# Expert input rows on ScalarE's DMA queue, and three placements around a mixture of experts

## The chip, the cores and the metric

The kernel runs on one core of one Trainium2 chip. The metric is the device time of one execution in microseconds (us), as the median of several runs. PE is TensorE, DVE VectorE, ACT ScalarE, POOL GpSimd and SP SyncE. Each of them has an instruction stream of its own, which it works through in order; SP does nothing here but issue DMAs, and ACT and POOL issue DMAs among their other instructions.

## The reference, cut to what matters

Two layers run over 256 latent and 256 context tokens of width 1024. Each layer has attention, an output projection, a layer norm, and then a mixture of 16 experts, two of which work on each token:

```
x   = layer_norm(ALPHA * x + (1 + gate1) * o, ln1_g, ln1_b)       # o: output projection
u   = x * (1 + scale2) + shift2                                   # input rows of the experts
affinity = sigmoid(u @ w_router);  best group, then its top 2 experts;  gate = affinity / their sum
f   = sum over the two experts of  gate * ((silu(u @ w1[e]) * (u @ w3[e])) @ w2[e])
x   = layer_norm(ALPHA * x + (1 + gate2) * f, ln2_g, ln2_b)
```

In layer 0 both streams go through the experts (512 tokens). In layer 1 only the latent tokens do (256), and only they are returned.

## The kernel before, in words

**Tokens and experts.** A layer's tokens stand in tiles of 128 rows: `n_out` is 4 in layer 0 and 2 in layer 1. An expert works on a block of at most `CAP` tokens, 96 in layer 0 and 64 in layer 1, whose rows it fetches from DRAM by their numbers; an expert with more tokens than that would be worked off inside an `If` (L1354), which is not entered with these inputs. The weights of the experts, 6 MB each, stream through SP's queue from beginning to end (L1302, pieces of 1 MB; L1293, two halves of one).

**End of the output projection.** For each tile of tokens `residual` (L915 to L917) makes the sum `z` out of the projection `oacc` and the stream `xs`. `post_norm` then takes the statistics (`BN_STATS`, L245, and on ACT the root of the variance, `sd<-mv`, L251, called `keep["root"]` in the code), forms the experts' input rows `u2` on DVE (L924, L943; the profile calls this tile `u`), writes them to the DRAM tensor `u2d` by a DMA (L944), and forms the normalised row `xs` on ACT (L942). Two DVE operations (L946, L949) turn that row into the residual that the experts' results are to be added to, and a DMA on ACT's queue (L950) writes it to the DRAM tensor `ysum`. `router` transposes `z` on PE, copies the transposes out of PSUM on ACT (`zt<-ztp`, L961) and multiplies them with the router's weights into `lgt`; L971 to L973 on DVE make the affinities' arguments `aff` of it. For the last tile a dummy sigmoid (L940) loads ACT's function table beforehand. The sigmoid of all affinities is one instruction (L1007), and it waits for the last tile's `aff`.

**Routing and the first gather.** DVE works out who goes where (up to `posm`, the place of each token at each expert). For expert 0 the one-hot matrix `oh` (L1125) is multiplied with token numbers on PE (`ix`, L1132 and L1134), DVE makes indices of it (`ii`, L1148, `keep["found"]`), POOL zeroes `xg` (L1150) and gathers the rows of `u2d` (L1151). The gather must wait for all writes to `u2d`. Behind it on POOL stand the gate parts (L1087 and its neighbours, which fill `auxg`), and behind them PE's `ix` sums of the gates (L1134). DVE's residual operations that are listed as `late` stand behind `ii`. Some weight loads wait for a mark that POOL sets behind a gather.

**The stages of a mixture.** For each expert: up-projection (`ha` for the first 64 slots, L1178, and in layer 0 `hb` for the other 32, L1184), gating on ACT (SiLU, L1205 and L1209) and DVE (L1206 and L1210), transposes of the gated rows on PE (`tp`, L1163) that ACT copies out (`gT`, L1166), down-projection (`ya`, `yb`), gate and addition to `ysum` by a scattering DMA (L1247).

**Its tail.** Behind the last expert's up-projection the rows of `ysum` are read back (`yu`, L1454). ACT casts each tile's row to a head (`parts`, L1456), and DVE (tile 0) or POOL (the others, in layer 0) subtracts the head from the row (L1457), so that head and rest can be summed exactly on PE together with the last expert's result (`racc`, L1488 and L1498). Dummy products (`warm`, L202, into `spare`) stand on PE ahead of the transposes of the last gated rows.

**What sets the order.** Each engine's instructions stand in the order in which a scheduler places them at build time; `order(a, b, ...)` puts a behind b, and `tc.high_priority()` takes a stretch ahead. In addition each DMA issued by SP or ACT takes one of eight completion semaphores in turn, and waits until the last DMA on the same semaphore has landed (the `DMAHW` waits in the listings below). A DMA issue that waits holds up all that stands behind it on its engine.

Of the kernel before, what the change touches and what calls it, by code (L numbers as in the profile page):

```python
# [17 lines left out]
F32 = mybir.dt.float32  # L18
# [4 lines left out]
AF = mybir.ActivationFunctionType  # L23
ALU = mybir.AluOpType
# [85 lines left out]
def layers(ctx: ExitStack, tc: tile.TileContext, x_in, x_ctx, c_in, w_in, w_out, w_ada, rows_in, lnv, sink, gains, rpbp,  # L110
# [344 lines left out]
    def pre_moe(l, sb, sr):  # L455
# [5 lines left out]
        with ExitStack() as st, ExitStack() as su:  # L461
# [458 lines left out]
            def post_norm(t, z):  # L920

                _, gg, bb = mods[t // 2]
                mean, rstd = stats([z[:, h] for h in half])
                u2 = tmp.tile([P, D], F32, tag="u2", name="u2")  # L924
                V.scalar_tensor_tensor(out=u2[:, half[0]], in0=z[:, half[0]], scalar=mean, in1=gg[:, half[0]],
                                       op0=ALU.subtract, op1=ALU.mult)
                if t < n_out - 1:
                    y, nmr = rstd()
                    for n in range(2):
                        if n:  # L930
                            V.scalar_tensor_tensor(out=u2[:, half[n]], in0=z[:, half[n]], scalar=mean, in1=gg[:, half[n]],
                                                   op0=ALU.subtract, op1=ALU.mult)
                        V.scalar_tensor_tensor(out=u2[:, half[n]], in0=u2[:, half[n]], scalar=y, in1=bb[:, half[n]],
                                               op0=ALU.mult, op1=ALU.add)
                    S.activation(out=xs[:, t], in_=z, func=AF.Identity, scale=y, bias=nmr)
                else:
                    V.scalar_tensor_tensor(out=u2[:, half[1]], in0=z[:, half[1]], scalar=mean, in1=gg[:, half[1]],
                                           op0=ALU.subtract, op1=ALU.mult)
                    y, nmr = rstd()
                    order(S.activation(out=sm.tile([P, 1], F32, tag="sd", name="sigmoid"), in_=epsc, func=AF.Sigmoid),  # L940
                          keep["root"], mybir.DependencyClass.NoSync)
                    S.activation(out=xs[:, t], in_=z, func=AF.Identity, scale=y, bias=nmr)  # L942
                    V.scalar_tensor_tensor(out=u2, in0=u2, scalar=y, in1=bb, op0=ALU.mult, op1=ALU.add)  # L943
                keep["u2 written"] = nc.sync.dma_start(u2d[t * P:(t + 1) * P], u2)  # L944

                d = V.scalar_tensor_tensor(out=xs[:, t], in0=xs[:, t], scalar=ALPHA, in1=lg, op0=ALU.mult, op1=ALU.mult)  # L946
                if t in (2, n_out - 1):
                    keep.setdefault("late", []).append(d)
                V.scalar_tensor_tensor(out=xs[:, t], in0=lb, scalar=ALPHA, in1=xs[:, t], op0=ALU.mult, op1=ALU.add)  # L949
                S.dma_start(ysum[l][t * P:(t + 1) * P], xs[:, t])  # L950
                return z, mean, y

            def router(t, z, mean, y):
                r = t // 2
                for hf in range(2):
                    tp = ps.tile([P, 512], F32, tag="s", name="ztp")
                    for k in range(4):
                        kt = hf * 4 + k
                        T.transpose(tp[:, k * P:(k + 1) * P], z[:, kt * P:(kt + 1) * P], ident)
                    zt = tmp.tile([P, 512], F32, tag="zt", name="zt")  # L960
                    d = S.copy(zt, tp)  # L961
                    if hf and t == n_out - 1:
                        order(d, keep["root"], mybir.DependencyClass.NoSync)
                    for k in range(4):
                        kt = hf * 4 + k
                        keep["logits"] = T.matmul(lgt[:, t * NE:(t + 1) * NE], zt[:, k * P:(k + 1) * P], wsc[:, r, kt],
                                                  start=(kt == 0), stop=(kt == 7))

                lo = aff[:, t]
                ms = sm.tile([P, NE], F32, tag="ms", name="ms", bufs=2)  # L970
                V.tensor_scalar(out=ms, in0=wsum[:, 0, r], scalar1=mean, scalar2=None, op0=ALU.mult)  # L971
                V.tensor_tensor(out=lo, in0=lgt[:, t * NE:(t + 1) * NE], in1=ms, op=ALU.subtract)
                V.scalar_tensor_tensor(out=lo, in0=lo, scalar=y, in1=wsum[:, 1, r], op0=ALU.mult, op1=ALU.add)  # L973
# [128 lines left out]
    class Experts:  # L1102
# [53 lines left out]
        def transposed(self, src, n, tag, after=None):  # L1156

            kk, cap, pool = n // P, self.cap, self.m1 if tag == "x" else self.m2
            out_ = pool.tile([P, kk, cap], F32, tag=tag + "T", name=tag + "T")
            for a in range(0, kk, 4):  # L1160
                tp = self.ps2.tile([P, 512], F32, tag="tp", name="tp")
                for k in range(4):
                    d = T.transpose(tp[:, k * P:k * P + cap], src[:cap, (a + k) * P:(a + k + 1) * P], ident[:cap, :cap])  # L1163
                    if after is not None:
                        order(d, after, mybir.DependencyClass.NoSync)
                (V.tensor_copy if a else S.copy)(out_[:, a:a + 4], tp.rearrange("p (k c) -> p k c", k=4)[:, :, :cap])  # L1166
            return out_

        def side_by_side(self, acc, x, kts, w, n):
# [30 lines left out]
        def gated(self, acc):  # L1200
# [2 lines left out]
            n = min(self.cap, 64)  # L1203
            hs = self.m2.tile([P, DE], F32, tag="hs", name="hs")
            S.activation(out=hs[:n], in_=a[:n], func=AF.Silu)  # L1205
            V.tensor_tensor(out=hs[:n], in0=hs[:n], in1=a[64:64 + n], op=ALU.mult)  # L1206
            for hf in range(2) if b is not None else ():
                o, c, k = hs[64:self.cap, hf * 256:hf * 256 + 256], 64 * hf, self.cap - 64
                S.activation(out=o, in_=b[c:c + k, 0:256], func=AF.Silu)  # L1209
                V.tensor_tensor(out=o, in0=o, in1=b[c + 32:c + 32 + k, 0:256], op=ALU.mult)  # L1210
            return hs

        def result(self, ht, pieces):
# [36 lines left out]
    def moe(l, ringb, gen, rt, u2d, aff, nt, sb, ahead):  # L1250
        cap = CAP[l]
        with ExitStack() as st:
# [197 lines left out]
                     for pool, tag in ((ringu, "wu"), (ringu, "wu"), (ringb[0], "wb"), (ringu, "wu"))[:nt]]  # L1450
            parts = [u[:, i * D:i * D + D] for u in parts for i in range(2)]
            g = ex.gates(toks[-1][1])
            heads, rests = [], []
            for t in range(nt):  # L1454
                keep["sums"] = nc.sync.dma_start(ys[t], ysum[l][t * P:(t + 1) * P])
                heads.append(S.copy(parts[2 * t], ys[t]))  # L1456
                rests.append((G if t in REST_G[l] else V).tensor_tensor(out=parts[2 * t + 1], in0=ys[t],  # L1457
                                                                     in1=parts[2 * t].bitcast(F32),
                                                                     op=ALU.subtract))
            spare = ps1.tile([P, 512], F32, tag="hb", name="spare")  # L1460
            warm(WARM[4], spare, keep["product"])
            acc = ex.result(ex.transposed(hs, DE, "g", after=keep["warm"]), piece)
            last_product = keep["product"]
            ahead(order)
            yl = ringb[1].tile([P, 2048], F32, tag="wb", name="yl")
# [160 lines left out]
```

## Time and profile before

| | us |
|---|---|
| three runs | 1144.89, 1145.07, 1151.78 |
| median | 1145.07 |
| profiled execution | 1139.29 |
| its span in the trace | 1137.5 |
| PE busy | 1017.5 (89%) |
| layer 0: end of the output projection and routing | 313 to 343 |
| layer 0: experts | 343 to 615 |
| layer 0: tail | 615 to 640 |
| layer 1: end of the output projection and routing | 850 to 882 |
| layer 1: experts | 882 to 1102 |

The profiled execution is 5.78 us shorter than the median of the runs, and 1.8 us longer than its own span. A row of the timeline gives start and duration in us, engine, line, operation and tiles (out<-in), and in brackets how long the engine stood idle ahead of it and what ended that. A row of the windows gives the busy time of each engine in a stretch, then the granted TensorE clock (1.00 is full speed), the busy share of the DMA engines (which can come out a little above 1) and GB/s. Layer 1's experts run at the pace of the weight loads, layer 0's at the pace of PE.

### The profile page before, as it was taken

To read this page: it belongs to the slowest core of one execution; us is meant where nothing else is said; L and a number is where in the kernel's file an instruction comes from. 1 tells how busy PE (TensorE), PEld (TensorE's weight loads), DVE (VectorE), ACT (ScalarE), POOL (GpSimd) and SP (SyncE) were. 2 spreads that over 40 slices of the span, in tenths; PEclk is the share of its full clock that TensorE was granted. 3 is DMA by queue.
4 is the path that set the end of the run, shared out by engine and by line. 5 is a ranking of instruction groups with operands and counts; after the bars stand their busy time and mean duration, and the time that the engine had idled before them with its cause. 6 is when DMAs were issued, how large, how long until landed. Compare 5 with 4: busy or idle time off the path is not lost. (4 is left out here: it accounts for less than half of the span.)

```text
span 1137.5 us, 21098 instructions
## 1 busy us (share of the span) xinstructions
PE 1017.5 (89%) x8683; PEld 597.6 (53%) x8684; DVE 522.4 (46%) x1221; ACT 332.6 (29%) x688; POOL 257.0 (23%) x238
## 2 busy tenths in 40 slices
PE   6998999999959999999996799989985999778775
PEld 4676767677844444444442577667773334222222
DVE  2424756665962344444434634566875222111115
ACT  1324568465221011011111533456631101000002
POOL 3000000100013433433324200001002455434142
PEclk9998999999968999999999899999996999989987
DMA  9845353866798999999995326674398999999992
GB/s 315 319 154 172 135 150 107 310 223 249 279 395 281 374 376 363 368 369 338 353 379 203 115 94 212 212 239 149 139 402 301 367 391 398 398 390 389 407 388 82
DMA packets 65617, 320.93 MB, mean 282 GB/s; under 512 B 14702, under 2 KB 18894, under 8 KB 35048
## 3 DMA queue, kind: packets, MB, share of 16 engines
q1 hardware_dynamic: 48576, 289.21, 66.9%
q0 software_dynamic: 11136, 23.30, 7.8%
q10 hardware_dynamic: 5800, 6.97, 1.8%
q8 instruction: 71, 1.16, 0.4%
q14 instruction: 34, 0.28, 0.1%
HBM read 310.40 MB, written 18.15 MB: 289 GB/s over the span
## 5 line engine op out<-in xcount | busy, mean ns | idle before, releaser
L1178 PE MATMUL ha<-w,xT 128*32 128x512 f32 (+1 forms) x1512 | 252.5, 613 | 17.7 <-DMA w<-in_w_dram 17.2
L1178 PEld LDWEIGHTS ha<-w,xT 128*32 128x32 f32 (+1 forms) x1512 | 74.8, 123 | 161.9 <-issue 122.4
L1205 ACT ACTIVATE hs<-ha 64x512 f32<-64x512 f32 x32 | 18.9, 590 | 403.6 <-PE ha L1178 403.6
L1178 PE MATMUL ya<-w,gT 128*32 128x512 f32 (+1 forms) x768 | 124.8, 597 | 3.2 <-DVE y L1225 1.6
L222 PE MATMUL pj<-wl,u 128*128 128x512 f32 (+2 forms) x256 | 97.8, 383 | 0.0
L221 PE MATMUL pj<-wh,u 128*128 128x512 f32 (+2 forms) x256 | 93.1, 389 | 4.8 <-ACT wh L211 3.2
L223 PE MATMUL pj<-wh,u 128*128 128x512 f32 (+2 forms) x256 | 92.6, 376 | 0.0
L1150 POOL MEMSET xg<- 96x1024 f32 (+1 forms) x32 | 30.1, 946 | 214.5 <-PE tp L1163 134.8
L1247 POOL DMA_INDIRECT ysum<-y,ii x30 | 44.2, 1474 | 149.2 <-DVE y L1228 98.0
L1225 DVE TENSOR_TENSOR y<-ya,gt 64x512 f32<-64x512 f32 x60 | 41.3, 688 | 77.9 <-PE ya L1178 70.1
L542 ACT ACTIVATE p<-s,nm 128x512 f32<-128x512 f32 (+1 forms) x96 | 59.2, 625 | 26.7 <-DVE nm L538 12.0
L212 DVE TENSOR_TENSOR wl<-w,wh 128x1024 fp32r<-128x1024 f32 x36 | 43.7, 1221 | 50.3 <-ACT wh L211 50.2
L1206 DVE TENSOR_TENSOR hs<-hs,ha 64x512 f32<-64x512 f32 x32 | 22.1, 689 | 95.0 <-ACT hs L1205 94.7
L531 DVE TENSOR_REDUCE mx<-s 128x1 f32<-128x512 f32 (+1 forms) x80 | 54.2, 687 | 18.0 <-PE s L516 10.5
L1178 PEld LDWEIGHTS ya<-w,gT 128*32 128x32 f32 (+1 forms) x768 | 33.3, 119 | 55.0 <-issue 46.8
L1184 PE MATMUL hb<-w,xT 128*32 128x256 f32 x1008 | 61.1, 379 | 0.0
L221 PEld LDWEIGHTS pj<-wh,u 128*128 128x128 f32 x256 | 48.8, 195 | 19.5 <-issue 4.5
L211 ACT CAST wh<-w 128x1024 fp32r<-128x1024 f32 x36 | 37.5, 1049 | 69.9 <-DMA w<-in_w_in_dram 35.8
L222 PEld LDWEIGHTS pj<-wl,u 128*128 128x128 f32 x256 | 49.7, 194 | 10.2 <-issue 1.6
L564 PE MATMUL o<-vt,pt 128*64 128x64 f32 x1280 | 52.7, 227 | 1.8 <-ACT pt L490 1.1
L223 PEld LDWEIGHTS pj<-wh,u 128*128 128x128 f32 x256 | 49.1, 192 | 9.1 <-issue 0.8
L555 PE MATMUL ptp<-cst,p 128*128 128x128 f32 x320 | 50.6, 279 | 3.4 <-ACT p L542 3.1
(295 smaller groups left out, 1699.4 us busy)
## 6 DMA issues: line engine op xcount, KB each, us to landing
w<-in_w_dram SPq DMA_DIRECT2D x164, 1024.0 KB
w<-in_w_ada_dram SPq DMA_DIRECT2D x44, 1024.0 KB
w<-in_w_dram SPq DMA_DIRECT2D x52, 512.0 KB
w<-in_w_in_dram SPq DMA_DIRECT2D x16, 1024.0 KB
w<-in_w_out_dram SPq DMA_DIRECT2D x8, 1024.0 KB
early<-in_w_ada_dram SPq DMA_DIRECT2D x4, 1024.0 KB
y<-modd POOLq DMA_DIRECT2D x6, 512.0 KB, 4.9
u2d<-u SPq DMA_DIRECT2D x6, 512.0 KB
```

What stands on the lines that cost most here:

```text
L212: keep["split"] = d = eng.tensor_tensor(out=lo, in0=w, in1=h.bitcast(F32), op=ALU.subtract)
L221: T.matmul(out_, ah, bh, start=start, stop=False)
L222: T.matmul(out_, ah, bl, start=False, stop=False)
L223: keep["product"] = T.matmul(out_, al, bh, start=False, stop=stop)
L531: greatest = V.reduce_max(out=mx[:, :nb], in_=s.rearrange("p (b k) -> p b k", b=nb), axis=AX.X)
L542: power = S.activation(out=p_[:, c * w:(c + 1) * w], in_=s[:, c * w:(c + 1) * w], func=AF.Exp, scale=scale, bias=bk.nm[:, c, i:i + 1], acc ...
L555: T.transpose(tp[:, k * P:(k + 1) * P], p_[:, k * P:(k + 1) * P], ident)
L564: T.matmul(bk.o[q:q + 64, oc:oc + HD], pt[:, (c * nk + k) * P + q:(c * nk + k) * P + q + 64], vt[:, (2 * (nb - 1)) + k, v0:v0 + HD], start ...
L1178: keep["product"] = T.matmul(a[64 * m + t0:64 * m + t1], x[:, kt, t0:t1], w(m, kt), start=(kt == 0), stop=(kt == n - 1))
L1184: keep["product"] = T.matmul(b[c:c + self.cap - 64, 0:256], x[:, kt, 64:], w(m, kt)[:, hf * 256:hf * 256 + 256], start=(kt == 0), stop=(kt ...
L1225: V.tensor_tensor(out=out_[:n, half[m]], in0=a[64 * m:64 * m + n], in1=g[:n, half[m]], op=ALU.mult)
L1247: G.indirect_dma_start(dst, bass.IndirectOffsetOnAxis(ap=ii[:cap], axis=0), y[:cap], None, bounds_check=self.nt * P - 1, oob_is_err=False, ...
```

## The change

1. The DMA that writes a tile's `u2` to `u2d` is issued by ACT, no longer by SP: four writes in layer 0 and two in layer 1.
2. The dummy sigmoid with its table load stands behind the last copy `zt`, before between the root and that copy.
3. The residual operations that stand behind `ii` are those of the last two tiles. In layer 0 these are tiles 2 and 3 as before; in layer 1 tiles 0 and 1, before tile 1 alone.
4. The warm products and the transposes of the last gated rows are written ahead of the read-back. Each head's cast stands behind the copy `gT`, and a rest on DVE behind the last gating.

```diff
@@ post_norm, last tile @@
-                    order(S.activation(out=sm.tile([P, 1], F32, tag="sd", name="sigmoid"), in_=epsc, func=AF.Sigmoid),
-                          keep["root"], mybir.DependencyClass.NoSync)
+                    keep["sigmoid"] = S.activation(out=sm.tile([P, 1], F32, tag="sd", name="sigmoid"), in_=epsc,
+                                                   func=AF.Sigmoid)
                     S.activation(out=xs[:, t], in_=z, func=AF.Identity, scale=y, bias=nmr)
                     V.scalar_tensor_tensor(out=u2, in0=u2, scalar=y, in1=bb, op0=ALU.mult, op1=ALU.add)
-                keep["u2 written"] = nc.sync.dma_start(u2d[t * P:(t + 1) * P], u2)
+
+                keep["u2 written"] = S.dma_start(u2d[t * P:(t + 1) * P], u2)
...
-                if t in (2, n_out - 1):
+                if t >= n_out - 2:
                     keep.setdefault("late", []).append(d)
@@ router @@
                         order(d, keep["root"], mybir.DependencyClass.NoSync)
+                        order(keep["sigmoid"], d, mybir.DependencyClass.NoSync)
@@ transposed @@
-                (V.tensor_copy if a else S.copy)(out_[:, a:a + 4], ...)
+                keep["turned"] = (V.tensor_copy if a else S.copy)(out_[:, a:a + 4], ...)
@@ gated @@
-            V.tensor_tensor(out=hs[:n], in0=hs[:n], in1=a[64:64 + n], op=ALU.mult)
+            keep["gated"] = V.tensor_tensor(out=hs[:n], in0=hs[:n], in1=a[64:64 + n], op=ALU.mult)
...
-                V.tensor_tensor(out=o, in0=o, in1=b[c + 32:c + 32 + k, 0:256], op=ALU.mult)
+                keep["gated"] = V.tensor_tensor(out=o, in0=o, in1=b[c + 32:c + 32 + k, 0:256], op=ALU.mult)
@@ tail of a mixture @@
+            spare = ps1.tile([P, 512], F32, tag="hb", name="spare")
+            warm(WARM[4], spare, keep["product"])
+            ht = ex.transposed(hs, DE, "g", after=keep["warm"])
             heads, rests = [], []
             for t in range(nt):
                 keep["sums"] = nc.sync.dma_start(ys[t], ysum[l][t * P:(t + 1) * P])
                 heads.append(S.copy(parts[2 * t], ys[t]))
+
+                order(heads[-1], keep["turned"], mybir.DependencyClass.NoSync)
                 rests.append((G if t in REST_G[l] else V).tensor_tensor(...))
-            spare = ps1.tile([P, 512], F32, tag="hb", name="spare")
-            warm(WARM[4], spare, keep["product"])
-            acc = ex.result(ex.transposed(hs, DE, "g", after=keep["warm"]), piece)
+                if t not in REST_G[l]:
+                    order(rests[-1], keep["gated"], mybir.DependencyClass.NoSync)
+            acc = ex.result(ht, piece)
```

Line numbers of the changed kernel are 1 to 7 higher than those of before in the stretches concerned. In the listings `DMAHW7_49` is one of the eight completion semaphores, `Activation`, `PE`, `DVE` and `Pool` are those of the engines.

ACT at the end of layer 0's output projection, before: from the copies of the third tile's transposes to the first `ysum` write of the late tiles.

```order
L961 COPY zt<-ztp 128x512 [waits PE_49,Activation_49] x3
L251 ACTIVATE sd<-mv,epsc 128x1 [waits DVE_49]
L940 ACT_TABLE_LOAD
L940 ACTIVATE sigmoid<-epsc 128x1
L961 COPY zt<-ztp 128x512 [waits PE_49,Activation_49]
L942 ACTIVATE xs<-z,nmr,y 128x1024 [waits DMAHW7_49,DVE_49]
L1007 ACTIVATE aff<-aff 128x64 [waits DVE_49]
L950 DMA ysum_117<-xs 128x1024 [waits DMAHW7_49,DVE_49]
```

and of the change:

```order
L945 DMA u2d_2967<-u_3295 128x1024 [waits DMAHW6_49,DVE_49]
L962 COPY zt<-ztp 128x512 [waits PE_49,Activation_49] x3
L251 ACTIVATE sd<-mv,epsc 128x1 [waits DVE_49]
L962 COPY zt<-ztp 128x512 [waits PE_49,Activation_49]
L940 ACT_TABLE_LOAD
L940 ACTIVATE sigmoid<-epsc 128x1
L942 ACTIVATE xs<-z,nmr,y 128x1024 [waits DMAHW7_49,DVE_49]
L945 DMA u2d_2967<-u_3404 128x1024 [waits DMAHW5_49,DVE_49]
L1009 ACTIVATE aff<-aff 128x64 [waits DVE_49]
L951 DMA ysum_117<-xs 128x1024 [waits DMAHW7_49,DVE_49]
```

The table load has moved behind the last copy, and the last write of `u2d` now stands between the normalised row and the sigmoid of the affinities, with a wait on a completion semaphore. On SP the two writes are gone from between the weight loads. Layer 1 reads alike.

ACT in the tail of layer 0's experts, before:

```order
L1205 ACTIVATE hs<-ha 64x512
L1456 CAST parts<-yu 128x1024
L1209 ACTIVATE hs<-hb 32x256
L1456 CAST parts<-yu 128x1024 x2
L1209 ACTIVATE hs<-hb 32x256
L1166 COPY gT<-tp 128x384
L1471 CAST yl<-yt 96x512 x2
L1456 CAST parts<-yu 128x1024
```

and of the change:

```order
L1207 ACTIVATE hs<-ha 64x512
L1211 ACTIVATE hs<-hb 32x256 x2
L1168 COPY gT<-tp 128x384
L1461 CAST parts<-yu 128x1024 x3
L1478 CAST yl<-yt 96x512 x2
L1461 CAST parts<-yu 128x1024
```

Three casts that stood around the two gatings now stand behind the copy `gT`. PE's order is the same there but for the third tile's sums of heads and rests, which are woven differently with the others. In layer 1's tail the casts stood behind `gT` before, and the order has not changed.

DVE at the end of layer 1's output projection, before, rows from the last tile's residual to the affinities:

```order
L916 TENSOR_TENSOR z<-oacc,y 128x512
L946 SCALAR_TENSOR_TENSOR xs<-xs,xg 128x1024
L917 SCALAR_TENSOR_TENSOR z<-xs,z 128x512
...
L972 TENSOR_TENSOR aff<-lgt,ms 128x16
L949 SCALAR_TENSOR_TENSOR xs<-ln_8833,xs 128x1024
L245 BN_STATS st<-z 128x6
```

and of the change:

```order
L916 TENSOR_TENSOR z<-oacc,y 128x512
L917 SCALAR_TENSOR_TENSOR z<-xs,z 128x512
L245 BN_STATS st<-z 128x6
...
L974 TENSOR_TENSOR aff<-lgt,ms 128x16
L249 BN_AGGR mv<-st 128x2
```

Tile 0's two residual operations no longer stand among the last tile's; they follow `ii`, behind the routing.

More of the change, by code (lines that the diff above doesn't have):

```diff
@@ L1165, in transposed @@
                         order(d, after, mybir.DependencyClass.NoSync)
-                (V.tensor_copy if a else S.copy)(out_[:, a:a + 4], tp.rearrange("p (k c) -> p k c", k=4)[:, :, :cap])
+                keep["turned"] = (V.tensor_copy if a else S.copy)(out_[:, a:a + 4], tp.rearrange("p (k c) -> p k c", k=4)[:, :, :cap])
             return out_
```

## Prediction

> **What bounds the kernel now.** I read the windows by stage first, then in the timeline the three stretches that the change touches, then the waits there. Here are the steady middle of each mixture, the stretches before its first gather, and the pause behind layer 1's gather.
>
> ```profile
> core 0: us, PE busy (x) PEld busy (x) DVE busy (x) ACT busy (x) POOL busy (x), PEclk, DMA share, GB/s
> 400.00:450.00 50.00, 49.68 (x615) 21.89 (x611) 20.28 (x44) 6.59 (x15) 18.90 (x12) 1.00 1.01 372
> 950.00:1050.00 100.00, 84.00 (x384) 30.94 (x384) 17.55 (x44) 8.06 (x20) 41.62 (x30) 0.93 1.02 396
> 313.00:334.00 21.00, 12.20 (x87) 10.14 (x85) 17.27 (x74) 4.23 (x7) 0.00 (x0) 0.66 1.02 421
> 850.00:877.00 27.00, 14.36 (x95) 11.16 (x95) 17.81 (x73) 6.68 (x11) 2.39 (x7) 0.67 0.95 362
> 863.00:869.00 6.00, 0.95 (x11) 0.69 (x10) 4.44 (x19) 0.00 (x0) 0.00 (x0) 0.75 1.03 427
> 877.00:882.00 5.00, 5.00 (x20) 1.42 (x18) 0.21 (x2) 0.00 (x0) 3.87 (x5) 0.73 0.11 27
> ```
>
> Layer 0's experts fill PE (49.68 of 50), so the tail behind them and the start before them count fully. Layer 1's experts fill the DMA engines (share 1.02, 396 GB/s); what counts there is when the weight stream starts. Before both gathers the DMA engines are full as well (421 and 427 GB/s), though PE and DVE are not. Between 877 and 882 they stand nearly idle (27 GB/s): the stream starts again only behind that pause.
>
> **Layer 0's tail.**
>
> ```profile
> 612.77 1.91 PE L1184 MATMUL hb<-w,xT 128*32 128x256 f32 x32
> 616.09 0.69 DVE L1444 CAST oht<-tp 96x512 fp32r<-96x512 bf16 x1
> 619.46 1.04 ACT L1456 CAST parts<-yu 128x1024 fp32r<-128x1024 f32 x1 [5.85 <-DMA yu<-ysum]
> 622.05 4.68 POOL L1457 TENSOR_TENSOR parts<-yu,parts 128x1024 fp32r<-128x1024 f32 x2 [7.31 <-ACT parts L1456]
> 623.25 0.38 ACT L1209 ACTIVATE hs<-hb 32x256 f32<-32x256 f32 x1
> 623.66 0.43 DVE L1210 TENSOR_TENSOR hs<-hs,hb 32x256 f32<-32x256 f32 x1 [1.45 <-ACT hs L1209]
> 624.14 2.72 PE L202 MATMUL spare<-zeros 128*128 128x256 bf16 x12 [9.11 <-DVE hs L1210]
> 627.47 0.48 ACT L1166 COPY gT<-tp 128x384 f32<-128x384 f32 x1 [3.84 <-PE tp L1163]
> 632.32 1.05 PE L1184 MATMUL yb<-w,gT 128*32 128x256 f32 x16
> 633.30 2.59 PE L1488 MATMUL racc<-parts,identr 128*128 128x512 f32 x10
> 1112.38 1.49 PE L202 MATMUL spare<-zeros 128*128 128x256 bf16 x12
> ```
>
> `hb` is complete at 614.68, but ACT, in order, stands 5.85 us at a cast that waits for the read-back; the last gating comes out at 624.09, and PE stands idle for 9.11. With the casts behind `gT`, the two SiLU (0.38 each) can run from 614.7 to 615.45. DVE is free at 616.78 and does its two products (0.43 each) by 617.65. PE starts at 617.7 in place of 624.14: **-6.4**. The casts then follow `gT`, which ends at 621.55: three of 1.04 end at 622.6, 623.6 and 624.7. POOL takes 2.34 for each rest, so the second and third tile's are done at 626.0 and 628.4. PE leaves `yb` at 626.97 and wants the third tile's rest after about ten sums of 0.26, at 629.6. The move is thus covered by down-projection and sums, with 1.2 us to spare; with that cover gone it costs up to one rest, 2.3. The bounds are -4.0 (a rest on the path) and -7.7 (the warm products in 1.49, as in layer 1, not 2.72).
>
> **Layer 0's first gather.**
>
> ```profile
> 319.52 1.28 DVE L943 SCALAR_TENSOR_TENSOR u<-u,y,xg 128x1024 f32<-128x1024 f32 x1
> 321.76 0.33 SPq L944 DMA_DIRECT2D u2d<-u  x1
> 321.86 0.26 ACT L1007 ACTIVATE aff<-aff 128x64 f32<-128x64 f32 x1 [0.98 <-DVE aff L973]
> 334.29 0.56 DVE L1125 TENSOR_TENSOR oh<-cst,posm 128x384 bf16<-128x384 f32 x1 [0.60 <-DMA u2d<-u]
> 335.21 1.04 POOL L1151 DMA_INDIRECT xg<-u2d,ii  x1 [34.27 <-DMA w<-in_w_dram]
> 336.58 0.21 PE L1132 MATMUL ix<-cbf 128*96 128x6 bf16 x1 [7.81 <-PEq L1354]
> 338.65 0.41 PE L1134 MATMUL ix<-auxg,oh 128*96 128x6 bf16 x4 [1.86 <-POOL auxg L1087]
> 854.35 0.33 ACTq L950 DMA_DIRECT2D ysum<-xs  x1
> ```
> ```profile
> SPq L944 <- DMA w<-in_w_dram: 6.6, 3, 3.4
> ```
> ```profile
> q10 hardware_dynamic: 144, 0.52, 25.6%
> ```
> ```profile
> L1354 PEldq COMPARE_BRANCH  x2: 378/3250/6121, 330.1 to 865.5; - x2
> ```
>
> The last rows are ready at 320.80. Their write is issued at 321.76, since SP waited for a weight load on the same semaphore (6.6 us over three such waits). It lands just before 334.29, 12.5 us later, behind the weights queued on SP; the gather follows at 335.21. On ACT's queue the nearest row is a `ysum` write of the same size: issued at 854.35, all its 144 packets (0.52 MB) lie between 858 and 863 while weights fill SP's queue, 8.6 us in all. The semaphore wait remains, now on ACT, so the issue stays at about 321.7 and the write lands at 330.35; the gather comes at 331.2, 4.0 earlier.
>
> PE does not follow by so much. It passes a branch for 6.1 us from 330.1 (the larger of the two in the row), and `ix` starts behind that, at 336.58. PE then waited 1.86 for the gate parts on POOL, which end 3.4 behind the gather. They will end at 334.6, so L1134 can follow L1132 at once, at about 337.0 rather than 338.65: **-1.6**. Queued behind the write on ACT is L1007, on which the routing rests. It is ready at 321.86, and the issue before it (0.33) ends around 322.0, so it slips 0.2 to 0.4. Should the weight load land 1.2 later, L1007 slips 1.5; that gives a bound of +1.0. The other bound is -4.0, the gather's full shift. I take -1.6, the value of the nearest row, PE's branch.
>
> A rule of the Trainium skill speaks against this term. "DMA: Bandwidth & Descriptors", section "Issuing engines are not separate DMA queues", says that all issuers' transfers run on the same 16 DMA engines and that issuing from several only saves sequencer time. Section "Queues, rings and completion order" of the same page says that each DMA engine takes turns between queue rows, packet by packet. The 8.6 us on ACT's queue agrees with the second; by the first alone this term would be 0.
>
> **Layer 1's first gather.**
>
> ```profile
> 851.06 1.22 DVE L946 SCALAR_TENSOR_TENSOR xs<-xs,xg 128x1024 f32<-128x1024 f32 x1
> 852.88 1.22 DVE L949 SCALAR_TENSOR_TENSOR xs<-ln,xs 128x1024 f32<-128x1024 f32 x1
> 855.30 1.28 ACT L940 ACT_TABLE_LOAD   x1
> 856.70 0.57 ACT L961 COPY zt<-ztp 128x512 f32<-128x512 f32 x1
> 858.72 0.33 SPq L944 DMA_DIRECT2D u2d<-u  x1
> 869.25 0.49 DVE L1125 TENSOR_TENSOR oh<-cst,posm 128x128 bf16<-128x128 f32 x2 [1.45 <-DMA u2d<-u]
> 869.96 1.02 POOL L1151 DMA_INDIRECT xg<-u2d,ii  x1 [44.16 <-DVE oh L1125]
> 871.13 1.00 SPq L1293 DMA_DIRECT2D w<-in_w_dram  x2
> 877.61 1.83 POOL L1150 MEMSET xg<- 64x1024 f32 x2 [4.97 <-SPq L1354]
> 881.98 0.37 SPq L1302 DMA_DIRECT2D w<-in_w_dram  x1
> ```
>
> DVE loses two operations of 1.22 ahead of the last statistics, about 2.2 us. The table load (1.28) moves behind the last `zt`, which then needn't wait for it. So the last rows are issued at about 856.5 in place of 858.72. With the same 8.6 us they land at about 865.0, and the gather goes at 865.8, 4.2 earlier. The moved operations run behind `ii`, four of 1.22 in all, while DVE would be waiting for `u2d`; if that cover were gone they would cost 2.4 more there.
>
> What follows is bound by bytes. The two halves (L1293) are issued behind the gather, and SP passes its branch only when all loads are in, at about 877.1; POOL's 4.97 of waiting ends there. From 850 to 877 the engines moved 27 x 362 GB/s = 9.77 MB. The same bytes take 22.9 us at 427 GB/s and 24.7 at 396, giving 872.9 and 874.7: -4.2 and -2.4. I take 404 GB/s, near the mixed stream's rate because two writes are in it: 24.2 us, 874.2, **-2.9**. The stream at 881.98 and the end behind it shift alike. The bounds are -0.3 (landing as late as now) and -4.3.
>
> **Sum.** -6.4 - 1.6 - 2.9 = -10.9. The profiled 1139.29 becomes 1128.4; the median lies 5.78 above it, so 1134.2, 0.9% below the median.
>
> **The rivals.**
>
> *Both gathers count in full.* If PE's branch slides with the routing, or is shorter with fewer loads in the queue, layer 0 gives -4.2, and layer 1 at 427 GB/s gives -4.2. For it: in 863 to 869 the engines reach that rate. Against it: nothing moves the branch's start. -6.4 - 4.2 - 4.2 = -14.8: 1130.3.
>
> *The other queue lands nothing earlier.* The engines are full either way, and this is what the first rule above would do. For it: share 1.02 before layer 0's gather. Against it: the `ysum` write's 8.6. Then only the tail and 0.3 remain: -6.7, 1138.4.
>
> *The writes starve on ACT's queue.* The `ysum` write had only weights beside it; a write that meets up to seven loads on SP's queue may get a small share. If it takes W from issue to landing, the time moves by -6.4 + (W - 12.6) + (W - 12.8), the two numbers being the span from the new issue to the present landing. Beyond W = 15.9 the kernel is slower; for 18 us it is +4.2, 1149.3. For it: ACT's queue gets but a quarter (25.6%) in its best stretch. Against it: 512 KB at a quarter of 421 GB/s need 5 us.
>
> *The tail's rests become the wait.* POOL's two rests are 1.2 us from deciding. If casts or copy come 3.6 later than worked out, PE waits 2.4: 1136.5.
>
> **How the numbers follow.** The forecast gets 0.46, since each term rests on a row. Both in full gets 0.20, no earlier landing 0.20, starving 0.07 and the rests 0.07. The range reaches from 1129.0 (both in full, with the tail at -7.7) to 1142.0 (no earlier landing, the tail at -4.0 and layer 0's front at +1.0, rounded up). About 1% is what a measurement of this kernel can tell: below 1133.6 or above 1156.5. The forecast lies at the lower border, 0.4 of it below; with most of the first rival that makes faster 0.40. Starving with W above 21.6 and mishaps unknown make slower 0.05; the rest is 0.55.
>
> **What would show it.** Right: the `hb` gating done near 617.7 and PE's wait there 2.7, not 9.1; the read-back's sums not held by `parts`; `u2d` landing 8 to 9 us after its issue; PE's `ix` in layer 0 still behind the branch but no longer behind `auxg`; the second gather of layer 1 some 3 us earlier. Wrong: writes on ACT's queue taking 12 us or more, L1007 held by the issue ahead of it, or layer 1's stream starting at 881 or later relative to an unshifted stage before it.

## The result, and the profile after

| | median us | runs | ratio to before | 95% interval |
|---|---|---|---|---|
| before | 1144.82 | 14 | | |
| changed | 1139.56 | 14 | 0.9948 | 0.9923 to 0.9974 |

The ratios rest on undisturbed executions; the only disturbed ones in this document are two of the ten of no_halves below, at 1659.79 and 2473.11 us.

The profiled execution of the changed kernel took 1135.72 us (span 1134.0) against 1139.29 (1137.5). The change makes the kernel about half a per cent faster, 5 to 6 us where 10.9 was forecast. The chain of gatings shows best where the time went: the first gating of `ha` in layer 0 came at 351.39 (before 353.94), the last at 615.42 (before 613.02), the first sum of heads and rests at 629.76 (633.30). So layer 0's experts started 2.55 earlier, ended 2.40 later, and the tail made up 5.9. Not all of the 2.55 is the change's: 0.45 lay ahead of it, 1.1 came through `ix` (below), and most of the rest is PE's first `ha` products, which took 9.98 us in place of 10.88. The granted clock had gone from 0.50 back to 1.00 some 3 us sooner there (at 343.8, for 347.2 before). How long that half-speed stretch lasts differs between executions: in the five profiles below with the writes on SP's queue and the halves in place, the first gating comes 78.45 to 80.05 us behind the first instruction of L251 in layer 0's post-norm, mostly for this reason.

The tail first, in the timeline of the changed kernel (PE, ACT, DVE and POOL rows in order of time):

```profile
617.03 0.42 PE L1445 MATMUL tp<-cbf,oh 128*96 128x128 bf16 x4
617.18 0.37 ACT L1211 ACTIVATE hs<-hb 32x256 f32<-32x256 f32 x1 [1.16 <-PE hb L1186]
619.21 0.42 DVE L1212 TENSOR_TENSOR hs<-hs,hb 32x256 f32<-32x256 f32 x1
619.66 0.37 ACT L1211 ACTIVATE hs<-hb 32x256 f32<-32x256 f32 x1 [2.11 <-DVE hs L1212]
620.54 2.72 PE L202 MATMUL spare<-zeros 128*128 128x256 bf16 x12 [3.09 <-DVE hs L1212]
624.31 2.94 ACT L1461 CAST parts<-yu 128x1024 fp32r<-128x1024 f32 x3
626.38 4.86 POOL L1464 TENSOR_TENSOR parts<-yu,parts 128x1024 fp32r<-128x1024 f32 x2 [9.24 <-ACT parts L1461]
629.76 2.36 PE L1495 MATMUL racc<-parts,identr 128*128 128x512 f32 x9
```

ACT no longer waits for the read-back ahead of the gating. PE stands idle for 3.09 in place of 9.11. One detail differs from the working: the second SiLU waits 2.11 for DVE's first product, so the two do not run back to back. The casts behind `gT` hide, as do POOL's rests: PE goes from `yb` into the sums without a wait.

Layer 0's front, POOL, DVE, ACT and PE:

```profile
321.50 0.33 ACTq L945 DMA_DIRECT2D u2d<-u  x1
321.87 0.26 ACT L1009 ACTIVATE aff<-aff 128x64 f32<-128x64 f32 x1 [1.45 <-DMA w<-in_w_dram]
329.08 2.34 DVE L947 SCALAR_TENSOR_TENSOR xs<-xs,xg 128x1024 f32<-128x1024 f32 x2
331.35 2.35 DVE L950 SCALAR_TENSOR_TENSOR xs<-ln,xs 128x1024 f32<-128x1024 f32 x2
330.50 4.12 POOL L1153 DMA_INDIRECT xg<-u2d,ii  x1 [30.00 <-DVE xs L947]
337.10 0.41 PE L1136 MATMUL ix<-auxg,oh 128*96 128x6 bf16 x4 [1.25 <-POOL auxg L1089]
344.09 1.83 POOL L1152 MEMSET xg<- 96x1024 f32 x2 [6.89 <-SPq L1356]
597.27 1.05 PE L1180 MATMUL ha<-w,xT 128*32 128x512 f32 x4 [0.48 <-DMA w<-in_w_dram]
599.75 4.88 PE L1180 MATMUL ha<-w,xT 128*32 128x512 f32 x26 [1.43 <-DMA w<-in_w_dram]
```

By the completion semaphores in the trace, the last write of `u2d` landed at 329.55, 8.05 us after its issue, in place of 12.5. The gather followed at 330.50, 4.7 earlier. But it took 4.12 in place of 1.04: it ended at 334.62, 0.92 behind the last of the late residual operations (331.35 + 2.35 = 333.70). And POOL left the branch at 344.09, no earlier than before (343.80). At the end of the stage PE now waits for weights, which it did not do before:

```profile
PEld ha L1180 <- DMA w<-in_w_dram: 3.0, 2, 2.3
PE ha L1180 <- DMA w<-in_w_dram: 1.9, 2, 1.4
```

These are the waits between 585 and 615 (us in total, times, longest); the same view of before has no wait for `w` there. Layer 1's front:

```profile
855.87 0.33 ACTq L945 DMA_DIRECT2D u2d<-u  x1
861.89 2.34 DVE L947 SCALAR_TENSOR_TENSOR xs<-xs,xg 128x1024 f32<-128x1024 f32 x2
864.15 2.34 DVE L950 SCALAR_TENSOR_TENSOR xs<-ln,xs 128x1024 f32<-128x1024 f32 x2
864.60 2.80 POOL L1153 DMA_INDIRECT xg<-u2d,ii  x1 [40.88 <-DVE xs L947]
867.54 1.84 SPq L1295 DMA_DIRECT2D w<-in_w_dram  x2
876.25 1.83 POOL L1152 MEMSET xg<- 64x1024 f32 x2 [7.17 <-SPq L1356]
```

The last write is issued 2.85 earlier and lands after 7.9 us; the gather starts 5.4 earlier and ends 3.6 earlier, again 0.9 behind the late operations (866.49). POOL leaves the branch only 1.36 earlier, though the stage ahead of the change had already been 2.07 earlier (the first instruction of that post-norm's L251, a table load, at 831.55 for 833.62). From there to the end of the pause it is 44.70 us in place of 44.00.

So two theories. **Theory 1**: the bytes decide. In both layers the pause ends when all transfers have landed, whenever the gather went, and in layer 0 the stream is late at the end; of the change only the tail counts. **Theory 2**: the earlier gathers count, and the waits for weights belong to that one execution.

### The profile page after: what moved, and what is told of

It reads as the page before. It is cut to its first block, busy times and chain, and to the rows that moved or that the text cites. A ratio compares the mean times of both kernels' runs of the same rounds, so it can differ in the third digit from the quotient of the medians.

```text
span 1134.0 us, 21098 instructions
## 1 busy us (share of the span) xinstructions
PE 1015.9 (90%) x8683; PEld 599.1 (53%) x8684; DVE 522.2 (46%) x1221; ACT 332.3 (29%) x688; POOL 262.0 (23%) x238
## 5 line engine op out<-in xcount | busy, mean ns | idle before, releaser
L1180 PE MATMUL ha<-w,xT 128*32 128x512 f32 (+1 forms) x1512 | 255.6, 619 | 17.8 <-DMA w<-in_w_dram 17.6
L1180 PEld LDWEIGHTS ha<-w,xT 128*32 128x32 f32 (+1 forms) x1512 | 77.4, 124 | 161.8 <-issue 124.1
L1180 PE MATMUL ya<-w,gT 128*32 128x512 f32 (+1 forms) x768 | 127.2, 597 | 3.8 <-DVE y L1227 1.6
L542 ACT ACTIVATE p<-s,nm 128x512 f32<-128x512 f32 (+1 forms) x96 | 59.2, 625 | 27.9 <-DVE nm L538 12.5
L1180 PEld LDWEIGHTS ya<-w,gT 128*32 128x32 f32 (+1 forms) x768 | 34.6, 119 | 56.5 <-issue 48.4
L221 PEld LDWEIGHTS pj<-wh,u 128*128 128x128 f32 x256 | 48.9, 195 | 18.1 <-ACT u L653 3.9
L1153 POOL DMA_INDIRECT xg<-u2d,ii x32 | 37.0, 1157 | 81.4 <-DVE xs L947 70.9
L564 PE MATMUL o<-vt,pt 128*64 128x64 f32 x1280 | 53.4, 229 | 2.5 <-ACT pt L490 1.1
L222 PEld LDWEIGHTS pj<-wl,u 128*128 128x128 f32 x256 | 49.7, 194 | 10.1 <-issue 1.6
L366 PE MATMUL ada<-w,csil 128*32 128x256 f32 x640 | 51.0, 392 | 4.0 <-DVE qkC L492 2.6
```

Of the source, the lines that this page charges most:

```text
L221: T.matmul(out_, ah, bh, start=start, stop=False)
L222: T.matmul(out_, ah, bl, start=False, stop=False)
L366: T.matmul(acc[32 * g:32 * g + 32, 0:256], csil[:, 2 * u + k], w[:, k * 1024 + g * 256:k * 1024 + g * 256 + 256], start=(k == 0), stop=(k ...
L542: power = S.activation(out=p_[:, c * w:(c + 1) * w], in_=s[:, c * w:(c + 1) * w], func=AF.Exp, scale=scale, bias=bk.nm[:, c, i:i + 1], acc ...
L564: T.matmul(bk.o[q:q + 64, oc:oc + HD], pt[:, (c * nk + k) * P + q:(c * nk + k) * P + q + 64], vt[:, (2 * (nb - 1)) + k, v0:v0 + HD], start ...
L1180: keep["product"] = T.matmul(a[64 * m + t0:64 * m + t1], x[:, kt, t0:t1], w(m, kt), start=(kt == 0), stop=(kt == n - 1))
```

## The experiments

The table puts all profiles side by side. Times are us from the first instruction of L251 in layer 0's post-norm (a table load, 12.8 ahead of the first root; "behind L251" and "behind the root" below count from it) or, for layer 1, from the first product of its output projection. "Pause ends" is the start of POOL's zeroing of `xg` (L1150) behind the branch; the weight stream follows 3 to 5 later. The last column is the time from the last gating of `ha` to the first sum (L1488). Each ratio below is the recorded one, to runs of the kernel before on the same chip. The medians of those runs go from 1144.48 to 1147.20, so medians of different chips don't compare, and a ratio is not the quotient of two medians (for tail_only that would be 0.9935, not 0.9950).

| run | rows on | gather ends, layer 0 | pause ends | last gating | gather ends, layer 1 | pause ends | tail |
|---|---|---|---|---|---|---|---|
| before | SP | 62.35 | 69.90 | 339.12 | 47.30 | 53.94 | 20.28 |
| tail_only | SP | 62.50 | 69.73 | 337.52 | 48.16 | 54.47 | 15.03 |
| thin_before | SP | 62.75 | 70.06 | 339.03 | 48.25 | 54.92 | 23.23 |
| rows_on_sp | SP | 63.07 | 70.19 | 339.12 | 46.66 | 54.49 | 12.86 |
| rows_on_sp_more | SP | 62.87 | 69.92 | 337.66 | 46.60 | 54.46 | 14.59 |
| changed | ACT | 61.17 | 70.64 | 341.97 | 45.80 | 54.65 | 14.34 |
| after_again | ACT | 61.28 | 71.45 | 339.64 | 45.07 | 54.53 | 12.85 |
| after_more | ACT | 62.36 | 71.13 | 340.87 | 46.01 | 54.61 | 15.82 |
| front_only | ACT | 62.36 | 71.30 | 340.54 | 44.57 | 53.55 | 22.59 |
| thin_after | ACT | 61.79 | 70.74 | 340.05 | 46.16 | 54.88 | 12.84 |
| late_behind_gather | ACT | 58.86 | 71.26 | 339.80 | 42.62 | 53.78 | 12.84 |
| no_halves | ACT | 61.89 | 67.74 | 337.49 | 44.71 | 50.42 | 14.91 |
| sp_no_halves | SP | 62.89 | 67.08 | 337.68 | 45.67 | 50.39 | 17.22 |
| tail_no_halves | SP | 62.61 | 66.81 | 337.33 | 47.06 | 51.78 | 18.38 |

**after_again** is the changed kernel, profiled a second time.

> The changed kernel once more, for a second profile. In the first one the first gating of layer 0's experts came 2.55 us earlier than before and the last one 2.40 later: from first to last gating 264.0 us in place of 259.1, with PE waiting for weights in the last two experts. Theory 1 (the weight stream of layer 0 ends too late to let the earlier start count): again 262 to 265, with PE waiting for weights there. Theory 2 (that execution was an odd one): 259 as before, and the gain at the front stands at the end.

From first to last gating 261.9 us, just under the range of Theory 1, and again a wait for weights (PE 1.4, its weight loads 2.8 in all). Theory 1 in kind; at 1131.36 us this execution was a quick one all the same.

**tail_only**, the fourth part alone on the kernel before:

```diff
+            spare = ps1.tile([P, 512], F32, tag="hb", name="spare")
+            warm(WARM[4], spare, keep["product"])
+            ht = ex.transposed(hs, DE, "g", after=keep["warm"])
             heads, rests = [], []
...
+                order(heads[-1], keep["turned"], mybir.DependencyClass.NoSync)
...
+                if t not in REST_G[l]:
+                    order(rests[-1], keep["gated"], mybir.DependencyClass.NoSync)
+            acc = ex.result(ht, piece)
```

> The kernel before with the fourth part of the change alone (casts of the rows read back behind the last gating). Both theories: from the last gating of ha to the first sum of heads and rests 14.3 us in place of 20.3, all 6.0 of it in the end time: 5 to 6 us faster than before, ratio 0.995. Rival (the later rests become a wait in the sums): 3 us or less.

1137.62 us, ratio 0.9950 (0.9929 to 0.9971): all of the changed kernel's gain.

**front_only**, the changed kernel with those lines taken back, so parts 1 to 3 alone:

> The changed kernel with the fourth part undone: writes on ACT's queue, late rows and sigmoid table alone. Theory 1 (stream and bytes take back what the earlier gathers bring): first gating of layer 0 2 us earlier than before, last one within 1 of before or later, the time within 1 us of before, ratio 0.998 to 1.003. Theory 2 (the local gains count): last gating of layer 0 2 us earlier, time 2 to 4 us less, ratio 0.997.

1144.58 us, ratio 1.0006 (0.9981 to 1.0031). Parts 1 to 3 bring nothing that can be measured (the interval leaves room for 2.2 us). The first gating came 1.1 later behind the root than before, not 2 earlier; its rows (timeline, POOL and PE) show why:

```profile
333.15 4.54 POOL L1153 DMA_INDIRECT xg<-u2d,ii  x1 [30.80 <-DVE ii L1150]
344.94 1.51 PE L1165 MATMUL tp<-cst,xg 96*128 96x96 f32 x8 [2.20 <-DMA xg<-u2d,ii]
346.62 1.84 POOL L1152 MEMSET xg<- 96x1024 f32 x2 [6.49 <-SPq L1356]
```

The gather takes 4.54, its rows land late, and PE waits 2.20 for them ahead of the first transposes; in after_more it waits 1.96. In the profile of the changed kernel above the rows were there in time. ACT's queue has a part in this. The issue of the last write waits there for a weight load on its semaphore, and the sigmoid of the affinities, with all the routing, stands behind it:

```profile
324.93 0.26 ACT L1009 ACTIVATE aff<-aff 128x64 f32<-128x64 f32 x1 [2.65 <-DMA w<-in_w_dram]
```

That is 49.61 behind L251, for 47.96 before; it is 47.3 to 48.2 in the seven profiles with rows on SP and 48.4 to 49.6 in the seven with rows on ACT. The late operations follow `ii` and slip with it, so the gather ends where it did before (62.36 for 62.35). Its rows land at 69.48 all the same, for 67.18 before; why is open. So what the earlier write brings is gone before the experts begin in some executions, and goes to the weights in the others.

**late_behind_gather**, the changed kernel with the late rows behind POOL's mark:

```diff
-                for d in keep.pop("late"):
-                    order(d, keep["found"], mybir.DependencyClass.NoSync)
                 mark = mark_after(first_gather)
+                for d in keep.pop("late"):
+                    order(d, mark, mybir.DependencyClass.Sync)
```

> The changed kernel with the late residual rows on DVE behind the mark that POOL sets after the first gather, not behind ii. Theory (the gather's work on POOL stands still while DVE works on the late rows): the gather takes 1.0 us in both layers in place of 4.1 and 2.8 and ends near 331.6 and 865.7. Rival (it waits for the landing of the rows or for its queue): 4.1 and 2.8 again. For the time: within 1 us of the changed kernel if bytes bind behind the gather; 2 to 3 us faster if the gather does.

1139.85 us, ratio 0.9950 (0.9924 to 0.9976), the same as the changed kernel. POOL's rows in layer 0, DVE's beside them, then POOL's in layer 1:

```profile
331.86 1.05 POOL L1153 DMA_INDIRECT xg<-u2d,ii  x1 [30.79 <-DMA u2d<-u]
332.96 1.52 POOL L1089 CAST auxg<-gate 128x32 bf16<-128x32 f32 x2
334.32 2.50 POOL L1091 TENSOR_TENSOR gate<-gate,auxg 128x32 f32<-128x32 f32 x2
```
```profile
333.06 2.43 DVE L947 SCALAR_TENSOR_TENSOR xs<-xs,xg 128x1024 f32<-128x1024 f32 x2 [2.31 <-POOL mark L1313]
335.42 2.49 DVE L950 SCALAR_TENSOR_TENSOR xs<-ln,xs 128x1024 f32<-128x1024 f32 x2
```
```profile
858.73 1.03 POOL L1153 DMA_INDIRECT xg<-u2d,ii  x1 [39.47 <-DMA u2d<-u]
861.31 1.15 POOL L1089 CAST auxg<-gate 128x32 bf16<-128x32 f32 x1
870.92 1.83 POOL L1152 MEMSET xg<- 64x1024 f32 x2 [6.11 <-SPq L1356]
```

The gather takes 1.05 and 1.03 again, and now the gate parts beside the late rows are the slow ones: a cast of `auxg` in layer 1 takes 1.15, where the changed kernel and the kernel before show 0.27 to 0.29. POOL's work stands while DVE runs these operations, whichever came first. "SBUF — State Buffer", section "Who interferes with whom" of the Trainium skill says that a DVE instruction with two SBUF inputs contends with a GpSimd instruction that reads SBUF; the late operations have two such inputs, and these rows agree. The second finding weighs more: both gathers ended 2 to 3 us earlier than in the changed kernel, and the pauses ended where they had (71.26 and 53.78). In layer 1 the halves, issued behind the gather, did land earlier with it (868.4, 51.3 behind the first product, for 54.1), but now the two `ysum` writes of the late rows came last, at 869.2 and 870.4, and the pause ended 0.5 behind them. In layer 0 the last of them landed at 344.9, and POOL went on at 345.31. The order of the transfers changed, their end did not.

**thin_before** and **thin_after** leave out four of layer 0's 96 weight loads, and with them those pieces' part of the result:

```diff
                 i = len(recent)
+                if l == 0 and i in (30, 40, 50, 60):
+                    units[loading[i]] = units[loading[i - 1]]
+                    recent.append(recent[-1])
+                    return
```

> The kernel before without four of layer 0's weight loads (pieces 30, 40, 50 and 60 of 96; the piece ahead of each is used twice, so four pieces' part of the result is left out). It gives the stream 4 MB, some 11 us, to spare. From first to last gating of layer 0 259.1 us as before, by either theory; last gating 337.5 to 339 us behind the first root of layer 0's post-norm.

> The changed kernel with the same four loads left out. Theory (the weight stream takes back what the earlier start of layer 0 brings): no wait for weights, 259.1 us from first to last gating in place of 264.0 and 261.9, and the last gating 336.5 to 337.5 behind the first root, 1 to 2 earlier than with the same loads left out of the kernel before. Rival (PE's own pace or clock): 262 to 264 again, last gating 339.5 to 342 behind the root.

From first to last gating 259.07 and 259.36: with the four loads left out, the long waits of the changed kernel's first two profiles are gone. That alone does not show the stream as their cause. The first gating of thin_after came late (80.69 behind L251), and front_only, after_more and late_behind_gather, where it came as late (80.4 to 81.5), have 259.35 to 259.36 with all their loads. Better evidence is no_halves below: its first gating stands where the changed kernel's did (77.92 for 77.94), its pause ends 2.9 us earlier, and it takes 259.57 in place of 264.04. The other half of the expectation missed: the last gating came 340.05 behind the root, 1.0 later than in thin_before, since the first one was already 0.7 late behind a gather of 4.20 and a wait for its rows. The stream is thus one of two places where the front's gain ends.

**rows_on_sp** and **rows_on_sp_more** put only the writes back:

```diff
-                keep["u2 written"] = S.dma_start(u2d[t * P:(t + 1) * P], u2)
+                keep["u2 written"] = nc.sync.dma_start(u2d[t * P:(t + 1) * P], u2)
```

> The changed kernel with the writes of the experts' rows back on SP's queue. Theory (the pause does not follow the gather): writes take 10 to 13 us again, the first gather of layer 1 ends 46 to 48 us behind the first product in place of 45, but the stream starts within 1 us of the changed kernel's in both layers, and the time is within 2 us of it. Rival (the earlier gather counts): 3 to 5 us slower than the changed kernel.

> The changed kernel with the writes of the experts' rows on SP's queue, again, in five rounds on the chip of the one before. Theory: within 1.5 us of the changed kernel. Rival (the queue costs): 2 to 4 us faster, and layer 0's stream starts 74 us behind the first root in place of 75.2.

1136.43 us, ratio 0.9924 (0.9895 to 0.9953), and 1140.16, ratio 0.9930 (0.9902 to 0.9958). With the writes slow again (12.6 to 13.2 us in layer 0, 10.0 and 10.1 in layer 1), nothing is lost; by its ratio rows_on_sp is 2.7 us faster than the changed kernel, where within 2 was expected, but the intervals overlap. In layer 1 the gather ends 0.6 to 1.6 later than in the three profiles of the changed kernel and the pause ends alike (54.5). In layer 0 the pause ends at 69.7 to 70.2 in all five profiles with rows on SP and the halves, and at 70.6 to 71.5 in the six with rows on ACT and the halves: the move makes it about 1.1 later. **after_more** ran on the same chip as rows_on_sp_more:

> The changed kernel once more beside the next one, in five rounds. Theory (only the fourth part brings time): ratio to before 0.993 to 0.997. Rival (the writes on ACT's queue cost some of it): the next kernel is 2 us or more faster than this one.

1140.76 us, ratio 0.9950 (0.9924 to 0.9975). The intervals overlap and the medians are 0.6 us apart, so that the queue costs the 2 us between the ratios is suggested at most.

**no_halves** is the changed kernel with `Y_UNIT = 0` in place of 1: nothing is loaded behind the first gather.

> The changed kernel without the piece that is loaded in two halves behind the first gather (Y_UNIT 0: that piece comes in the stream later). Theory (the pause behind the gather ends when all loads have landed, whenever the gather went): in layer 1 it ends near 49 us behind the first product of the output projection, when the loads ahead of the gather are in, in place of 54, and the stream starts near 53 in place of 58; 1 MB has to come later, so 2 to 3 us of it stay: ratio to before 0.990 to 0.994. Rival (the rows of the second gather or its slots hold it): stream at 57 to 58, time as the changed kernel or worse by the 1 MB.

1137.63 us as the median of all ten executions, ratio 0.9934 (0.9898 to 0.9971). The pause ends 3 us earlier in layer 0 (67.74) and 4 in layer 1 (50.42), though the gathers end within 1.5 us of the changed kernel's. POOL and SP in layer 1:

```profile
864.38 2.86 POOL L1153 DMA_INDIRECT xg<-u2d,ii  x1 [39.73 <-DVE xs L947]
872.95 1.83 POOL L1152 MEMSET xg<- 64x1024 f32 x2 [4.04 <-SPq L1356]
```
```profile
879.47 5.03 SPq L1304 DMA_DIRECT2D w<-in_w_dram  x4
```

**sp_no_halves** and **tail_no_halves** join this to rows_on_sp and to tail_only:

> The changed kernel with the writes on SP's queue and without the piece in two halves behind the first gather. Theory (the pause follows the landing of the loads and nothing else): the streams start 1.5 to 3 us earlier in layer 0 and 3 to 4 in layer 1; at the end 2 to 4 us less than with the halves, ratio to before 0.989 to 0.992. Rival (the 1 MB that comes later takes it all back): ratio as the kernel ahead of this one.

> The kernel before with the fourth part of the change alone and without the halves. Theory: as the kernel ahead of this one, ratio 0.989 to 0.992, since the first three parts bring nothing. Rival (late rows and table placement bring 2 us or more in layer 1): 0.992 to 0.995.

1137.93 us, ratio 0.9912 (0.9879 to 0.9944), and 1138.30, ratio 0.9917 (0.9889 to 0.9946). The first is the fastest of the study by its ratio, 0.9% under the kernel before; against the changed kernel's 0.9948 the intervals still overlap. Against the same kernels with the halves that is 1.4 to 3.8 us by the ratios, not the 5 to 7 of both layers' earlier streams; here too the intervals overlap. Part of the difference is in their tails, which are longer (17 to 18 us; the first `ya` products take 3.64 in both, 1.93 in the changed kernel). In both the granted clock stayed at 0.50 until 630, into the down-projection, while in the changed kernel it was back at 1.00 by 624, ahead of it. A window of sp_no_halves:

```profile
620.00:630.00 10.00, 8.09 (x48) 3.75 (x51) 2.02 (x3) 3.69 (x5) 2.81 (x2) 0.50 1.00 384
```

Why it stayed low is open. The pauses of these two runs also correct the expectation that they follow the landing of the loads and nothing else. SP had nothing left to wait for there, and the pause ended behind POOL's own work after the gather (gate parts and branch): 4.2 us behind the gather's end in layer 0 and 4.7 in layer 1, alike in both runs. POOL in layer 1, sp_no_halves and then tail_no_halves:

```profile
868.63 1.02 POOL L1153 DMA_INDIRECT xg<-u2d,ii  x1 [42.53 <-DVE oh L1127]
874.37 1.83 POOL L1152 MEMSET xg<- 64x1024 f32 x2 [3.05 <-DMA xg<-modd]
```
```profile
872.29 1.02 POOL L1151 DMA_INDIRECT xg<-u2d,ii  x1 [43.92 <-DVE oh L1125]
878.03 1.83 POOL L1150 MEMSET xg<- 64x1024 f32 x2 [3.05 <-DMA xg<-modd]
```

From the first product, the gather of sp_no_halves ends 1.39 earlier than that of tail_no_halves, and its pause ends 1.39 earlier too. In every profile with the halves the landings came later than POOL's work. So with the halves in place the pause follows the landings, as Theory 1 has it; without them an earlier gather begins to count.

## Why the prediction was half right

**The sign, the range and the tail held.** The range held because it had room for the second rival, which left both fronts out; of the three terms of the sum only one came true. The tail was forecast at -6.4. Alone it gives a ratio of 0.9950, 5.7 us of 1144.8 (3.3 to 8.1). From the end of `hb` to the first warm product it is 3.4 us in place of 9.5, so -6.0: that the second SiLU waits for DVE's first product (the 2.11 above) was missed. What PE waits for was named rightly, and the rests did not become the wait. Over all profiles the tail shrank by 8.1, from 22.0 (three with the old tail) to 13.9 (eight with the new one and the halves). Of that, 6.0 is the wait ahead of the warm products. The other 2.1 lies between them and the first sum and goes with the granted clock: that stretch took 7.7 us where the clock was at 1.00 throughout, 9.1 to 9.3 where it was back ahead of the down-projection, and 10.7 to 11.8 where it was not. In front_only PE ran the down-projection at half speed, in the changed kernel's second profile at full. The windows of those two, over the last gating and the first half of the down-projection:

```profile
core 0: us, PE busy (x) PEld busy (x) DVE busy (x) ACT busy (x) POOL busy (x), PEclk, DMA share, GB/s
625.86:629.86 4.00, 2.78 (x14) 2.10 (x14) 0.42 (x1) 0.69 (x2) 3.88 (x2) 0.50 1.01 427
629.86:633.86 4.00, 3.38 (x20) 1.08 (x22) 0.00 (x0) 0.48 (x1) 0.00 (x0) 0.50 0.11 45
```
```profile
615.44:618.44 3.00, 0.04 (x1) 0.00 (x0) 2.50 (x4) 0.50 (x2) 0.00 (x0) 1.00 0.33 76
618.44:622.44 4.00, 3.25 (x32) 2.03 (x35) 0.59 (x2) 1.98 (x3) 0.00 (x0) 1.00 0.97 381
```

That the old tail's idle stretch is what slows the clock is not shown: the kernel before idled 9.11 as well, and its clock was back at 1.00 ahead of the same products (1.92 us).

**Layer 0's front, -1.6, came to nothing, and its first steps were right.** Issue (321.50 for 321.7), landing (8.05 us for 8.6; the row behind that 8.6 lasted 9.15 by its completion semaphore) and start of the gather (330.50 for 331.2) fit. The start of `ix` behind the gate parts (L1134, now L1136: 337.10 for 337.0) fits by luck. Of its shift 0.45 lay ahead of the change (from the root it is 63.65 for 64.75), PE's branch did move (the first `ix` behind it at 335.64 for 336.58), and PE still waits 1.25 for the gate parts, which the text had done at 334.6. L1009 was held by the issue ahead of it (1.45 us here, 2.65 in front_only), one of the text's own signs of being wrong. Two steps failed. The text set the gather's price at its old 1.04 and laid the late rows under the wait for `u2d`; with the write early they lie under the gather instead, which stands still until they end. And the first sentence after the windows read layer 0's experts as filled by PE, so that an earlier start counts fully. The same row showed the DMA engines at a share of 1.01: the weight stream was as full as PE. The stream's restart hangs on the pause, not on PE, and it came later.

**Layer 1's front, -2.9, is 0: this step failed outright.** The issue came at 855.87, for about 856.5, but 2.07 of its 2.85 lay ahead of the change: from the output projection's first product it came 0.78 earlier. Over all profiles that point is 35.0 to 36.8 with the old order of DVE's operations and 33.0 to 34.8 with the new one, about the 2.2 of the text. The landing (7.9 us) fits. The step from the gather to the pause was wrong. The text let the loads end earlier because the engines would fill the same bytes in faster. The rate did come, 403 GB/s over the same 27 us counted from the first product, for the 404 of the text:

```profile
847.92:874.92 27.00, 12.98 (x103) 10.55 (x103) 18.16 (x72) 7.32 (x11) 4.17 (x7) 0.71 0.99 403
```

But the bytes were not the same. Up to the last landing 10.9 MB moved (27.81 us at 392 GB/s), for 9.8 before, since the weight stream was about one load (1 MB) less far when the stretch began; in the second profile it was 0.3 MB less far, so this differs between executions. And what landed earlier gave its place to something else: measured from the output projection's first product, the write landed at 42.2, 41.3 and 40.9 in the changed kernel, its second profile and front_only, in place of 45.5 and 46.3 (before, tail_only), and the last load ahead of the gather at 49.1, 49.2 and 48.3 in place of 48.0 and 48.7. The halves, then, were in at 53.0 to 54.1 in place of 53.4 and 54.0. That the earlier writes are what pushed the last load back is argued, not shown: the two ranges overlap, and on SP's queue both writes stood ahead of that load as well. The stream went on at 880.85, at a stage 2.07 earlier: past the 881 that the text named as a sign of being wrong. What did move the pause was 1 MB less ahead of it.

**The rivals.** The second one, no earlier landing, gave the nearest time (1138.4), for a reason that the trace refutes: the writes did land sooner (8.05 us behind their issue for 12.5 in layer 0, 7.9 for 10.4 in layer 1). Its outcome is that of the rule of the Trainium skill ("DMA: Bandwidth & Descriptors", section "Issuing engines are not separate DMA queues") that issuing on several engines saves sequencer time only: here single transfers land sooner or later by the queue, while the end of them all, with the halves, stays (53.6 to 54.9 us in layer 1 whichever queue). The starving of the writes did not happen (8 us), nor did the rests become the wait. What stays open is why layer 0's pause ends 1.1 later with the rows on ACT's queue.

## What to carry to other kernels

Where DMA engines are full ahead of a point that waits for all transfers, suspect that a transfer that lands sooner only trades places, as it did here; count the bytes that must land, and take some out, rather than reorder them, until another limit shows (here POOL's work behind the gather). When a wait goes, look at what had been hidden under it and now runs beside the next step on a shared resource, and at what stands behind an issue that you move to another engine. And where a stage shows both PE and DMA near 1.0, as layer 0's experts do, do not count an earlier start of PE alone in full.

## What the runs showed of the hardware

A gather issued by POOL takes 1.04 us by itself and 2.8 to 4.5 beside DVE operations on 128x1024 with two inputs in SBUF; it ended 0.9 behind the last of them in both layers. One of POOL's small casts went from 0.27 to 1.15 in the same company. After an idle stretch of some 9 us PE's granted clock stood at 0.50 for the next 8 us in front_only and the products there took nearly twice as long (3.64 us for 16 `ya` products, 1.93 in the changed kernel). The length of the idle stretch did not settle it: after 9.11 us in the kernel before those products took 1.92, after 3.5 us in sp_no_halves 3.64.
